# Three score tiles in the first attention too, value halves in whole tiles, and probability tiles in two pools

## The chip, the cores and the metric

The kernel runs on one core of one Trainium2 chip. The metric is the device time of one execution in microseconds; 2905.07 is the median of three executions of the kernel before. A change of about 0.2% can be told from none.

## What is computed

One block of a hybrid model, for 1024 tokens of width 1024 in fp32: a first feed-forward, a token mix, a second feed-forward, a final norm. The mix projects the normed tokens once and runs two attentions on the result. Cut to what matters here:

```python
proj = h @ w_in                                   # q, k, v of the first attention, q and six k/v of the second, gates
# first: differential attention, 8 heads, two score maps each, 128 query rows at a time
s = einsum('bqhcd,bkhcd->bhcqk', qb, k) * scale   # causal
p = softmax(s);  a = p[:, :, 0] - lam * p[:, :, 1]
o = rmsnorm(einsum('bhqk,bkhe->bqhe', a, v), head_gain) * (1.0 - lam_init)
# second: NSA, 16 heads in 2 groups: compressed, selected and window branch, mixed by gates
y_ns = g[..., 0:1] * o_cmp + g[..., 1:2] * o_slc + g[..., 2:3] * o_win
merged = sigmoid(g_a) * (y_da @ w_proj_da) + sigmoid(g_b) * (y_ns @ w_proj_nsa)
return merged @ w_out
```

## The kernel before

Everything up to the two attentions is projections and the first feed-forward. A projection is done as three products of high and low halves (`mm3`, L52 to L54: hi with whi, lo with whi, hi with wlo). So every operand is first split: ACT rounds the high half (L89), DVE subtracts it for the low half (L85). These two lines are helpers and carry many different tiles.

**The first attention** (`da_phase`) goes over eight heads and, in each, over four steps m of 256 queries, two blocks z of 128. A block has w = 128 (2m + z + 1) keys. For each block and each of the two maps, `scores` makes a score tile S on PE (L909) out of the keys kt and the queries qt, DVE adds the mask and takes the minimum nm (L916), ACT writes the exponential into a probability tile Pt (L918). POOL and DVE mix the two maps. One step later `da_pv` transposes the tiles on PE into a group tr (L964), splits it into th (ACT) and tl (DVE), and multiplies with the values vt into o (L991 to L993). `da_finish` copies o to ob and squares it to sq (ACT, L999 and L1001); `da_finish2`, a step later, sums sq on PE (tot, L1008), takes a reciprocal root by a chain of DVE, ACT (yr, yr, zr) and POOL (zr, zr, yr), scales ob on DVE (L1014), splits it into yo and stores it (syd).

Between the attention's steps stands **filler**: the projections of later heads, of gates and of the attention's output, cut into pieces (gm is their accumulator in PSUM). Weight tiles come by DMA (wst) and are split into whi and wlo, on ACT and DVE, at L1208 in the filler. `rope_pair` writes rotated queries and keys (rh, rl) to sq and sk in DRAM; `v_da_unit` transposes a head's projected values in two halves tb, splits them and stores them to sv. Keys, values and queries come back from there by DMA when their head begins (kt, vt, qt). All these DMAs are issued by one queue, SP's, one after another.

**The second attention** (`ns_phase`) is built alike: for each head and block a selected and a window score tile and their probability tiles Ps and Pw, transposed into th and tl of fp16.

**What sets the order.** The code records instructions; a scheduler then orders each engine's queue by priorities and by when pool buffers come free. The filler has a lower priority. Nothing in the code fixes where a DMA stands in SP's queue, so an edit of a pool reorders the queues around it. In the built program each engine's instructions, and SP's DMAs, stand in one fixed order.

**What the change touches.** `score_tile` has two modes. With `K.narrow`, a tile of up to 512 keys takes one PSUM bank, and there are three score tiles and three transposed groups; else a score tile takes two banks, and there are two of each. When the mode changes, both pools are closed and opened again in the other form over the same banks. Before, the first attention has `K.narrow` False and is always wide; the second is in both modes. `K.narrow` also chooses fp16 in `tr_split`. The pool mp has one buffer each of the tags rh and rl, of 4 KB a partition; a half of a head's values uses 2 KB of it. In the second attention the probability tiles are six buffers deep, in one pool.

Of the kernel before, what the change touches and what calls it, by code (L numbers as in the profile page):

```python
# [7 lines left out]
F32 = mybir.dt.float32  # L8
F32R = mybir.dt.float32r
F16 = mybir.dt.float16  # L10
# [8 lines left out]
P = 128  # L19
T = 1024  # L20
TB = 512
NTB = 2
# [21 lines left out]
def open_pool(K, ctx, name, bufs, psum=False, side=None):  # L44
    kw = {"space": PSUM} if psum else {}
    if side:
        kw["side"] = side
    return ctx.enter_context(K.tc.tile_pool(name=name, bufs=bufs, reuse_waits="tile", **kw))
# [35 lines left out]
def lo_of(nc, lo, src, hi):  # L84
    return nc.vector.tensor_tensor(out=lo, in0=src, in1=hi.bitcast(F32), op=ALU.subtract)  # L85


def split(nc, hi, lo, src):
    nc.scalar.activation(out=hi, in_=src, func=AF.Copy)  # L89
    return lo_of(nc, lo, src, hi)  # L90
# [37 lines left out]
def load_w(K, src):  # L128
    if K.fill is not None:
        return K.fill.take()  # L130
    return load_w_parts(K, src, 1)()


def load_w_parts(K, src, n):
    nc = K.nc
    st = K.wst.tile([P, KD, P], F32, tag="wst", name="wst")
    hi = K.whl.tile([P, KD, P], F32R, tag="whi", name="whi")
    lo = K.whl.tile([P, KD, P], F32R, tag="wlo", name="wlo")
    at = [0]

    def part():
        r = slice(at[0] * KD // n, (at[0] + 1) * KD // n)
        nc.sync.dma_start(out=st[:, r], in_=src[:, r])
        split(nc, hi[:, r], lo[:, r], st[:, r])
        at[0] += 1
        return hi, lo
    return part
# [495 lines left out]
def v_da_unit(K, h):  # L643
    nc = K.nc
    w = load_w(K, K.A["win"][C_VDA + h])
    for tb in range(NTB):
        ps = K.gm.tile([P, TB], F32, tag="gm", name="gm")
        yield from fill_gemm(K, ps, w, K.h[tb])
        vt = K.mp.tile([P, TB], F32, tag="m13", name="vt")
        nc.vector.tensor_tensor(out=vt, in0=ps, in1=K.R[tb], op=ALU.mult)  # L650
        tr = K.gm.tile([P, 4, P], F32, tag="gm", name="tr")
        for j in range(4):
            nc.tensor.transpose(tr[:, j], vt[:, j * P:(j + 1) * P], K.ident)
        vh = K.mp.tile([P, 4, P], F32R, tag="rh", name="vh")
        vl = K.mp.tile([P, 4, P], F32R, tag="rl", name="vl")
        split(nc, vh, vl, tr)
        for hl, t in ((0, vh), (1, vl)):
            nc.sync.dma_start(out=K.s_v[h][hl][:, tb * 4:tb * 4 + 4], in_=t.bitcast(F32))


def v_ns_unit(K, br):
# [297 lines left out]
def tr_split(K, blocks):  # L959
    nc = K.nc  # L960
    n = len(blocks) * P
    tr = K.tr.tile([P, TB], F32, tag="tr", name="tr")
    for b, src in enumerate(blocks):
        nc.tensor.transpose(tr[:, b * P:(b + 1) * P], src, K.ident)  # L964
    dt = F16 if K.narrow else F32R
    hi = K.tp.tile([P, TB], dt, tag="th", name="th")
    lo = K.tp.tile([P, TB], dt, tag="tl", name="tl")
    if K.narrow:
        nc.scalar.activation(out=hi[:, 0:n], in_=tr[:, 0:n], func=AF.Copy)  # L969
        nc.vector.tensor_tensor(out=lo[:, 0:n], in0=tr[:, 0:n], in1=hi[:, 0:n], op=ALU.subtract)  # L970
    else:
        split(nc, hi[:, 0:n], lo[:, 0:n], tr[:, 0:n])
    return hi, lo
# [104 lines left out]
def ns_scores(K, hd, m, qt, g, step):  # L1078
    nc = K.nc
    res = []  # L1080
    for i in (2 * m, 2 * m + 1):
        w = P * (i + 1)
        b0 = max(0, i - 4)
        ww = P * (i + 1 - b0)
        l = K.sm.tile([P, 2], F32, tag="l", name="l")
        nm = K.sm.tile([P, 2], F32, tag="nm", name="nm")
        qs = [t[:, (i % 4) * P:(i % 4 + 1) * P] for t in qt]
        p1 = K.pp.tile([P, 5 * P], F32, tag="P1", name="Pw")
        p0 = K.pp.tile([P, T], F32, tag="P0", name="Ps")
        scores(K, [(q, K.nk[g, 0], 0) for q in qs], w, K.slab[:, T - w:T], nm[:, 0:1], p0, l[:, 0:1])  # L1090
        mk = K.slab[:, T - ww:T] if i < 4 else K.wslab
        scores(K, [(q, K.nk[g, 1], b0 * P) for q in qs], ww, mk, nm[:, 1:2], p1, l[:, 1:2])
        nc.vector.reciprocal(out=l, in_=l)
        nc.vector.tensor_tensor(out=l, in0=l, in1=K.G[:, i, hd * 3 + 1:hd * 3 + 3], op=ALU.mult)  # L1094
        for p, n, c in ((p0, w, 0), (p1, ww, 1)):
            nc.gpsimd.tensor_scalar(out=p[:, 0:n], in0=p[:, 0:n], scalar1=l[:, c:c + 1], scalar2=P_NS,  # L1096
                                    op0=ALU.mult, op1=ALU.mult)
        res.append((p0, p1, b0))
        step()
    return res  # L1100
# [70 lines left out]
class Filler:  # L1171
# [58 lines left out]
    def step(self):  # L1230
        K = self.K
        K.gate = K.last
        self.due += self.rate
        while self.due >= 1.0 and self.done < self.target:
            self.due -= self.next()
        K.gate = None
# [102 lines left out]
def da_units(K, p):  # L1339
    return [lambda: rope_pair(K, C_QDA + 2 * p, K.s_q[p]), lambda: rope_pair(K, C_KDA + 2 * p, K.s_k[p]),  # L1340
            lambda: v_da_unit(K, 2 * p), lambda: v_da_unit(K, 2 * p + 1)]
# [15 lines left out]
B_NP = 6  # L1357
B_DT = 2
B_NT = 4
B_NO = 1  # L1360
LOW_DA = 20
LOW_NS = 100
PACE_DA = 16
# [3 lines left out]
def da_phase(K, cg):  # L1367
    nc = K.nc
    with ExitStack() as ctx:
        K.kp, K.vp, K.qp = open_pool(K, ctx, "dk", B_DK), open_pool(K, ctx, "dv", B_DV), open_pool(K, ctx, "dq", B_DQ)  # L1370
        K.nk, K.vv = {}, {}
        for n, f in enumerate(da_units(K, 0)[:2] + da_units(K, 1)):
            if n == 2:
                early = da_load_parts(K, 0)
            if n >= 2:
                next(early)
            if n == 5:
                q0 = da_queries(K, 0, 0)
            drain([f()])
        cg.close()  # L1380
        K.low = LOW_DA
        log_exp(K)
        K.pp, K.sm, K.tp, K.op = (open_pool(K, ctx, "dp", B_DP), open_pool(K, ctx, "dsm", 6), open_pool(K, ctx, "dt", B_DT),
                                  open_pool(K, ctx, "do", 1))
        K.narrow = False
        K.gm = open_pool(K, ctx, "gm1", 1, True, side="right")
        K.ops = open_pool(K, ctx, "o1", 1, True, side="right")
        pend = K.fin = None

        def finish(h, m, res):  # L1390
            if m % 2 == 0:
                K.o = K.ops.tile([P, TB], F32, tag="o", name="o")
            if K.fin:
                da_finish2(K, *K.fin)
                K.fin = None
            da_pv(K, h, m, res, K.o)
            if m % 2 == 1:
                K.fin = da_finish(K, h, m // 2, K.o)

        ng = NG_DA // 2  # L1400
        W = K.A["win"]
        units = []
        for p in (2, 3):
            cs = [[C_QDA + 2 * p, C_QDA + 2 * p + 1], [C_KDA + 2 * p, C_KDA + 2 * p + 1], [C_VDA + 2 * p], [C_VDA + 2 * p + 1]]
            units += [(f, [W[c] for c in ws]) for f, ws in zip(da_units(K, p), cs)]
        units += [(f, [W[C_GATE + c]]) for c, f in enumerate(gate_units(K, range(16)))]
        units += [(lambda d=d: pda_unit(K, d), [K.A["wda"][d]]) for d in range(KD)]
        fill = K.filler = Filler(K, units)
        for p in range(4):
            fill.pace(4 * (p + 1) if p < 2 else 8 + ng * (p - 1), PACE_DA)  # L1410
            for h in (2 * p, 2 * p + 1):
                if h:
                    da_load(K, h)
                for m in range(4):
                    qt = q0 if h + m == 0 else da_queries(K, h, m)
                    if h == 4:
                        ns_load_key(K, m)
                    res = da_scores(K, h, m, qt, fill.step)
                    if pend:
                        finish(*pend)  # L1420
                    pend = (h, m, res)
            fill.end()
        finish(*pend)
        with K.tc.high_priority(offset=-100):
            da_finish2(K, *K.fin)
        close_scores(K)


def ns_phase(K):
    nc = K.nc  # L1430
    K.low = LOW_NS
    with ExitStack() as ctx:
# [5 lines left out]
        K.kp = open_pool(K, ctx, "nk", 1)  # L1438
        K.pcp.append(open_pool(K, ctx, "npc1", 1))
        K.qp.append(open_pool(K, ctx, "nq1", 1))  # L1440
        K.tp, K.sm, K.pp, K.op = (open_pool(K, ctx, "nt", B_NT), open_pool(K, ctx, "nsm", 6), open_pool(K, ctx, "np", B_NP),
                                  open_pool(K, ctx, "no", B_NO))
        K.narrow = True
        K.gm = open_pool(K, ctx, "gm2", 1, True, side="right")
        K.ops = open_pool(K, ctx, "o2", 1, True, side="right")
        fill = K.filler
# [268 lines left out]
```

## Time and profile before

| | |
|---|---|
| median of 3 runs | 2905.07 us (2904.47 to 2907.5) |
| the profiled execution | 2906.79 us, its span 2905.0 us |
| mean granted clock of PE | 0.988 |
| PE busy in the span | 2791.6 us, 96% |
| first attention, 970 to 1478 us | PE busy 466.37 of 508, granted clock 0.97 |
| second attention, 1478 to 2068 us | PE busy 572.20 of 590, granted clock 0.99 |
| waits of PE for ACT's Pt, 970 to 1480 us | 11.1 us in 8 |
| waits of ACT's vh for the store of vh (sv) | 6.6 us in 3, the longest 5.5 |

The profile is of one execution; times are from the start of the span. In a row of the timeline stand start, length, engine, line, instruction and operands, and in brackets how long the engine had been idle before it and which instruction it then waited for. SPq is the DMA queue of SP: its length there is the issue, not the transfer. A row of waits gives the total, the number and the longest. PE's matmuls overlap, so the distance of two starts, not the length of one row, says what a matmul takes.

### The profile page before, as it was taken

The numbers are of one execution on the slowest core, as the hardware profiler recorded it, in microseconds if no ns is written. First come the engines' busy times: TensorE is split into PE (matmuls) and PEld (weight loads), VectorE is DVE, ScalarE is ACT, GpSimd is POOL, SyncE is SP. The second block draws the span as 40 slices with busy tenths as digits, with TensorE's granted clock in tenths as the row PEclk, the third lists the DMA queues.
The fourth block names the chain that finished last, engine by engine and source line by source line (L and its number), as shares of the span: only waits on it lengthen the run. The fifth ranks groups of instructions, "written<-read, shape, count | busy, mean of one in ns | idle before, by whom it ended". The sixth has DMA issues, their size and how long they took to land. (4 is left out here: it accounts for less than half of the span.)

```text
span 2905.0 us, 40199 instructions
## 1 busy us (share of the span) xinstructions
PE 2791.6 (96%) x14278; PEld 2056.3 (71%) x14278; DVE 1997.1 (69%) x3356; ACT 1371.3 (47%) x2351; POOL 785.8 (27%) x701
## 2 busy tenths in 40 slices
PE   8999999999999999989989999999999999999998
PEld 6644447887788778878867778888787854445886
DVE  7876866666688467667767777777433976676566
ACT  7533424442333245445556666677433654343443
POOL 3134321000045222322233333333242414233001
PEclk9999999999999999999999999999999999999999
DMA  4355448654446645444432226222843246444854
GB/s 163 122 201 187 168 170 279 220 182 141 152 178 213 222 150 179 164 164 159 154 121 84 89 80 204 88 88 81 311 150 123 74 148 222 162 174 170 294 181 145
DMA packets 212137, 476.12 MB, mean 164 GB/s; under 512 B 20832, under 2 KB 39520, under 8 KB 211936
## 3 DMA queue, kind: packets, MB, share of 16 engines
q1 hardware_dynamic: 211936, 473.55, 47.8%
q8 instruction: 112, 1.84, 0.3%
q14 instruction: 89, 0.73, 0.1%
HBM read 312.52 MB, written 160.96 MB: 163 GB/s over the span
## 5 line engine op out<-in xcount | busy, mean ns | idle before, releaser
L405 PEld LDWEIGHTS <-w 128*128 128x128 f16 x3024 | 297.1, 99 | 379.5 <-issue 28.6
L52 PE MATMUL gm<-hi,whi 128*128 128x512 f32 x880 | 352.2, 400 | 5.9 <-ACT whi L89 3.2
L54 PE MATMUL gm<-hi,wlo 128*128 128x512 f32 x880 | 349.2, 398 | 0.4 <-DVE wlo L85 0.3
L53 PE MATMUL gm<-lo,whi 128*128 128x512 f32 x880 | 348.8, 396 | 0.0
L405 PE MATMUL Y<-tf,w 128*128 128x512 f16 x1296 | 296.3, 383 | 17.8 <-DVE u L443 14.7
L909 PE MATMUL S<-kt,qt 128*128 128x320 f32 (+5 forms) x1152 | 268.9, 352 | 27.0 <-ACT Pt L918 11.1
L85 DVE TENSOR_TENSOR wlo<-st,whi 128x1024 fp32r<-128x1024 f32 x154 | 197.6, 1300 | 113.6 <-ACT whi L89 112.4
L916 DVE CUSTOM_DVE_ANT_0 S<-S,slab 128x896 f32<-128x896 f32 (+7 forms) x320 | 224.3, 710 | 55.6 <-PE S L909 50.6
L53 PE MATMUL acc<-wlo,whi 128*128 128x512 f32 (+1 forms) x628 | 244.1, 389 | 1.0 <-DVE wlo L85 1.0
L89 ACT ACTIVATE whi<-st 128x1024 fp32r<-128x1024 f32 x154 | 160.8, 1057 | 177.9 <-PE acc L54 110.0
L54 PE MATMUL acc<-whi,wlo 128*128 128x512 f32 (+1 forms) x628 | 242.8, 389 | 0.0
L52 PE MATMUL acc<-whi 128*128 128x512 f32 (+1 forms) x628 | 240.5, 387 | 0.0
L909 PEld LDWEIGHTS S<-kt,qt 128*128 128x128 f32 x1152 | 183.1, 190 | 43.9 <-ACT Pt L918 13.1
L970 DVE TENSOR_TENSOR tl<-tr,th 128x512 f16<-128x512 f32 (+2 forms) x304 | 183.8, 615 | 43.8 <-ACT th L969 42.5
L1096 POOL TENSOR_SCALAR Ps<-Ps,l 128x384 f32<-128x384 f32 (+7 forms) x128 | 101.1, 790 | 372.1 <-DVE l L1094 246.9
L969 ACT ACTIVATE th<-tr 128x512 f16<-128x512 f32 (+2 forms) x304 | 159.4, 540 | 79.6 <-PE tr L964 65.8
L52 PEld LDWEIGHTS gm<-hi,whi 128*128 128x128 f32 x880 | 169.0, 192 | 39.2 <-ACT whi L89 3.4
L405 PE MATMUL X<-h,w 128*128 128x512 f16 x864 | 195.3, 379 | 1.0 <-ACT s L415 1.0
L54 PEld LDWEIGHTS gm<-hi,wlo 128*128 128x128 f32 x880 | 168.4, 191 | 36.7 <-DVE wlo L85 1.5
L53 PEld LDWEIGHTS gm<-lo,whi 128*128 128x128 f32 x880 | 168.6, 192 | 30.9
L85 DVE TENSOR_TENSOR wlo<-wst,whi 128x1024 fp32r<-128x1024 f32 x103 | 138.4, 1346 | 49.4 <-ACT whi L89 39.5
L521 POOL TENSOR_TENSOR u<-u,u 128x512 f32<-128x512 f32 x36 | 52.0, 1444 | 344.3 <-DVE sa L102 162.1
(330 smaller groups left out, 6163.3 us busy)
## 6 DMA issues: line engine op xcount, KB each, us to landing
wst<-in_win_dram SPq DMA_DIRECT2D x55, 512.0 KB
sw<-w2s SPq DMA_DIRECT2D x44, 512.0 KB
st<-sw SPq DMA_DIRECT2D x88, 256.0 KB
st<-saT SPq DMA_DIRECT2D x88, 256.0 KB
a<-in_f1w_dram SPq DMA_DIRECT2D x36, 512.0 KB
a<-in_f2w_dram SPq DMA_DIRECT2D x36, 512.0 KB
st<-saB SPq DMA_DIRECT2D x66, 256.0 KB
qt<-sq SPq DMA_DIRECT2D x128, 128.0 KB
```

The source lines that it names most:

```text
L52: first = nc.tensor.matmul(out, lhsT=w[0][:, wk], rhs=x[0], start=start, stop=False, skip_group_check=skip)
L53: nc.tensor.matmul(out, lhsT=w[0][:, wk], rhs=x[1], start=False, stop=False, skip_group_check=skip)
L54: nc.tensor.matmul(out, lhsT=w[1][:, wk], rhs=x[0], start=False, stop=stop, skip_group_check=skip)
L85: return nc.vector.tensor_tensor(out=lo, in0=src, in1=hi.bitcast(F32), op=ALU.subtract)
L89: nc.scalar.activation(out=hi, in_=src, func=AF.Copy)
L405: K.mark = nc.tensor.matmul(o, lhsT=w[:, a, m * h + k], rhs=x[k][:, b], start=start and k == 0 and i == 0, stop=k == h - 1 and i == 2, ski ...
L521: nc.gpsimd.tensor_tensor(out=a, in0=a, in1=b, op=ALU.mult)
L909: K.last = nc.tensor.matmul(S[:, o:o + n], lhsT=q, rhs=k[:, k0 + c:k0 + c + n], start=i == 0, stop=i == 1)
L916: nc.vector.tensor_tensor_reduce(out=sv, in0=sv, in1=mv, scale=-0.125, scalar=BIG, op0=ALU.add, op1=ALU.min, accum_out=nm)
L969: nc.scalar.activation(out=hi[:, 0:n], in_=tr[:, 0:n], func=AF.Copy)
L970: nc.vector.tensor_tensor(out=lo[:, 0:n], in0=tr[:, 0:n], in1=hi[:, 0:n], op=ALU.subtract)
L1096: nc.gpsimd.tensor_scalar(out=p[:, 0:n], in0=p[:, 0:n], scalar1=l[:, c:c + 1], scalar2=P_NS, op0=ALU.mult, op1=ALU.mult)
```

## The change

It has three parts. (1) `v_da_unit` takes one tile for both halves of a head's high values and one for the low ones, in the same two tags, at its start, and writes each half into its part; the stores are as many and as large as before. A half then no longer waits until the first half is stored, but the next user of a tag waits for the stores of both halves. (2) The first attention sets `K.narrow` too, so its steps m = 0, 1 (up to 512 keys) are narrow and m = 2, 3 wide: two changes of the pools a head, 16 in all. A new flag `K.half` keeps the type of th and tl as it was in both phases. (3) The six probability buffers of the second attention become a pool of two and one of four, used in the same rotation; the selected tile comes ahead of the window tile in each, the pool of y goes ahead of the small one, and a pad of 1 KB shifts them in SBUF.

```diff
 def v_da_unit(K, h):
     w = load_w(K, K.A["win"][C_VDA + h])
+    vs = [K.mp.tile([P, NTB, 4, P], F32R, tag=t, name="vs") for t in ("rh", "rl")]
     for tb in range(NTB):
...
-        vh = K.mp.tile([P, 4, P], F32R, tag="rh", name="vh")
-        vl = K.mp.tile([P, 4, P], F32R, tag="rl", name="vl")
-        split(nc, vh, vl, tr)
-        for hl, t in ((0, vh), (1, vl)):
-            nc.sync.dma_start(out=K.s_v[h][hl][:, tb * 4:tb * 4 + 4], in_=t.bitcast(F32))
+        split(nc, vs[0][:, tb], vs[1][:, tb], tr)
+        for hl in range(2):
+            nc.sync.dma_start(out=K.s_v[h][hl][:, tb * 4:tb * 4 + 4], in_=vs[hl][:, tb].bitcast(F32))
@@ tr_split
-    dt = F16 if K.narrow else F32R
+    dt = F16 if K.half else F32R
...
-    if K.narrow:
+    if K.half:
@@ ns_scores
-        p1 = K.pp.tile([P, 5 * P], F32, tag="P1", name="Pw")
-        p0 = K.pp.tile([P, T], F32, tag="P0", name="Ps")
+        pool = K.pp[K.n_p % B_NP > 1]
+        K.n_p += 1
+        p0 = pool.tile([P, T], F32, tag="P0", name="Ps")
+        p1 = pool.tile([P, 5 * P], F32, tag="P1", name="Pw")
@@ da_phase
-        K.narrow = False
+        K.narrow, K.half = True, False
@@ ns_phase
-        K.tp, K.sm, K.pp, K.op = (open_pool(K, ctx, "nt", B_NT), open_pool(K, ctx, "nsm", 6), open_pool(K, ctx, "np", B_NP),
-                                  open_pool(K, ctx, "no", B_NO))
-        K.narrow = True
+        K.tp, K.op, K.sm = open_pool(K, ctx, "nt", B_NT), open_pool(K, ctx, "no", 1), open_pool(K, ctx, "nsm", 6)
+        open_pool(K, ctx, "npad", 1).tile([P, 256], F32, name="npad")
+        K.pp, K.n_p = [open_pool(K, ctx, "npa", 2), open_pool(K, ctx, "npb", B_NP - 2)], 0
+        K.narrow, K.half = True, True
```

Each engine has as many instructions as before, of the same shapes. Their order differs in the first attention and in the first steps of the second; from there on only buffer and line numbers differ. Three places follow, before and after. A number behind a name is a buffer's or a tile's.

The first is SP's queue during head 3, around a filler weight load (wst), the key loads of head 4 (kt from sk2) and the stores of a pair of rotated queries (rh, rl). Before:

```order
L1031 DMA kt_10792<-sk2_78 128x1x1024
L635 DMA sq3_75<-rh_9775 128x2x512 x2
L635 DMA sq3_75<-rl_9776 128x2x512
L1198 DMA wst_9905<-in_win_dram 128x1024
L928 DMA qt_10336<-sq1_73 128x1x256 x2
L1031 DMA kt_10794<-sk2_78 128x1x1024
L1198 DMA wst_9959<-in_win_dram 128x1024
```

After:

```order
L635 DMA sq3_75<-rh_9795 128x2x512 x2
L635 DMA sq3_75<-rl_9796 128x2x512
L927 DMA qt_10198<-sq1_73 128x1x256
L1199 DMA wst_9933<-in_win_dram 128x1024
L927 DMA qt_10198<-sq1_73 128x1x256
L927 DMA qt_10201<-sq1_73 128x1x256 x2
L1199 DMA wst_9987<-in_win_dram 128x1024
L635 DMA sq3_75<-rh_9976 128x2x512 x2
L635 DMA sq3_75<-rl_9977 128x2x512
L927 DMA qt_10369<-sq1_73 128x1x256 x2
L1030 DMA kt_10832<-sk2_78 128x1x1024
```

The weight load and the three stores now stand ahead of both key loads.

The second is around heads 3 and 4. On SP: the stores of the second half of head 6's values (sv6), the key loads of head 5 (kt from sk2) and one of the second attention's (kt from skv). Before:

```order
L1047 DMA kt_10806<-skv_84 128x1x1024
L1031 DMA kt_11307<-sk2_78 128x1x1024
L928 DMA qt_10941<-sq2_74 128x1x256 x2
L1031 DMA kt_11309<-sk2_78 128x1x1024
L658 DMA sv6_0_97<-vh_10557 128x512
L658 DMA sv6_1_98<-vl_10558 128x512
L1198 DMA wst_10577<-in_win_dram 128x1024
```

After:

```order
L657 DMA sv6_0_97<-vs_10415 128x512
L927 DMA qt_10986<-sq2_74 128x1x256
L1046 DMA kt_10846<-skv_84 128x1x1024
L657 DMA sv6_1_98<-vs_10416 128x512
L1199 DMA wst_10621<-in_win_dram 128x1024
L927 DMA qt_10989<-sq2_74 128x1x256 x2
L1030 DMA kt_11363<-sk2_78 128x1x1024
L1030 DMA kt_11365<-sk2_78 128x1x1024
```

Both stores now stand ahead of both key loads of head 5. On PE, from the last o of head 3 to the first o of head 4 (th with the new values vt). Before:

```order
L992 MATMUL o_10715<-tl_10925,vt_10166 128x128
L993 MATMUL o_10715<-th_10924,vt_10168 128x128
L909 MATMUL S_10989<-kt_10794,qt_10941 128x512 x2
L909 MATMUL S_11055<-kt_10792,qt_11044 128x320 x4
L653 MATMUL tr_10781<-ident_299,vt_10779 128x128 x4
L1008 MATMUL tot_11011<-sq_10936,ones_297 128x512
L964 MATMUL tr_11030<-ident_299,Pt_10810 128x128
L964 MATMUL tr_11030<-ident_299,Pt_10847 128x128 x2
L909 MATMUL S_11063<-kt_10794,qt_11047 128x320 x4
L964 MATMUL tr_11130<-ident_299,Pt_10948 128x128
L909 MATMUL S_11099<-kt_10792,qt_11044 128x384 x4
L991 MATMUL o_11010<-th_11034,vt_10796 128x256
```

After, the last o of head 3 is followed by 24 rows of filler on gm, of which the last two begin this piece, and the first o of head 4 comes after 18 further filler rows behind its end (22 in all behind tr):

```order
L53 MATMUL gm_10874<-lo_4958,whi_10617 128x512
L54 MATMUL gm_10874<-hi_4957,wlo_10618 128x512
L1007 MATMUL tot_11059<-sq_10984,ones_297 128x512
L963 MATMUL tr_11078<-ident_299,Pt_10850 128x128
L963 MATMUL tr_11078<-ident_299,Pt_10895 128x128 x2
L52 MATMUL gm_11015<-hi_5400,whi_10617 128x512
L53 MATMUL gm_11015<-lo_5401,whi_10617 128x512
L54 MATMUL gm_11015<-hi_5400,wlo_10618 128x512
L52 MATMUL gm_11015<-hi_5418,whi_10617 128x512
```

Before, score matmuls and transposes filled this stretch; now 46 matmuls of filler do.

The third is ACT where the second attention begins; ob, sq, yr, zr and yo are the last head's finish. Before:

```order
L89 ACTIVATE th_12889<-tr_12885 128x384
L999 ACTIVATE ob_12899<-o_12773 128x512
L1001 ACTIVATE sq_12901<-ob_12899 128x512
L155 ACTIVATE yr_12907<-m_12905 128x512
L156 ACTIVATE yr_12907<-yr_12907 128x512
L157 ACTIVATE zr_12908<-yr_12907 128x512
L89 ACTIVATE yo_12916<-ob_12899 128x512
L918 ACTIVATE Ps_12989,l_12986<-S_12996,nm_12987 128x128
L918 ACTIVATE Pw_12988,l_12986<-S_13001,nm_12987 128x128
L918 ACTIVATE Ps_13017,l_13014<-S_13018,nm_13015 128x256
L1208 ACTIVATE whi_13038<-wst_12623 128x1024
L918 ACTIVATE Pw_13016,l_13014<-S_13023,nm_13015 128x256
```

After (two more rows of Ps and Pw, of the first pair, stand just ahead of this piece):

```order
L1209 ACTIVATE whi_13149<-wst_12727 128x1024
L917 ACTIVATE Ps_13127,l_13125<-S_13129,nm_13126 128x256
L917 ACTIVATE Pw_13128,l_13125<-S_13134,nm_13126 128x256
L998 ACTIVATE ob_13003<-o_12877 128x512
L1000 ACTIVATE sq_13005<-ob_13003 128x512
L155 ACTIVATE yr_13011<-m_13009 128x512
L968 ACTIVATE th_13210<-tr_13206 128x384
L156 ACTIVATE yr_13011<-yr_13011 128x512
L968 ACTIVATE th_13222<-tr_13218 128x384
L157 ACTIVATE zr_13012<-yr_13011 128x512
L89 ACTIVATE yo_13020<-ob_13003 128x512
L917 ACTIVATE Ps_13157,l_13155<-S_13159,nm_13156 128x384
```

The exponentials of two pairs, and a weight split, moved ahead of ob; those of the third pair still stand behind yo, and two th of the second attention now stand inside the finish.

More of the change, by code (lines that the diff above doesn't have):

```diff
@@ L1359 @@
 B_NT = 4
-B_NO = 1
 LOW_DA = 20
```

## Prediction

> **What bounds the kernel now.** I read the page's busy table first, then the stretches of the differential-attention phase and its neighbours, then who waits for whom on PE there, and last the timeline at the longest of those waits.
>
> ```profile
> span 2905.0 us, 40199 instructions
> PE 2791.6 (96%) x14278; PEld 2056.3 (71%) x14278; DVE 1997.1 (69%) x3356; ACT 1371.3 (47%) x2351; POOL 785.8 (27%) x701
> ...
> 970.00:1478.00 508.00, 466.37 (x2414) 392.15 (x2413) 343.81 (x701) 237.88 (x480) 134.44 (x133) 0.97 0.48 165
> 1478.00:2068.00 590.00, 572.20 (x3872) 469.62 (x3873) 444.30 (x1148) 391.31 (x898) 186.88 (x258) 0.99 0.34 114
> 1191.00:1295.00 104.00, 89.08 (x449) 75.08 (x449) 67.75 (x143) 46.78 (x99) 28.31 (x28) 0.91 0.50 178
> 1288.00:1301.00 13.00, 10.42 (x41) 8.64 (x41) 7.62 (x13) 3.57 (x8) 5.03 (x4) 0.74 0.46 159
> ```
>
> The columns of the last four rows are the stretch, its length, the busy time of PE, PEld, DVE, ACT and POOL, the granted PE clock, the DMA share and GB/s. PE bounds the program, and the change alters neither the number nor the shape of any instruction, so time can come only from PE's idle time and from its slow clock. The first row of a stretch is the phase that the change reorders: PE stands still for 508 - 466.4 = 41.6 us, and the clock costs 508 x 0.03 = 15. Of that, the 104 us from 1191 hold 14.9 idle and 104 x 0.09 = 9.4 of clock; the next phase, whose pools the change lays out anew, idles only 17.8 in 590.
>
> ```profile
> PE S L909 <- ACT Pt L918: 11.1, 8, 5.6
> PE S L909 <- DMA kt<-sk: 4.4, 2, 4.1
> PE o L991 <- ACT th L89: 3.9, 1, 3.9
> PE o L991 <- DMA vt<-sv: 2.8, 1, 2.8
> PE S L909 <- ACT Ps L918: 8.8, 2, 8.0
> ```
>
> (The last row is of the next phase; the numbers are total, times, longest.) So the loss is a few long waits, not many short ones: one of 5.6 makes half of the eleven on score tiles. The kt wait (4.1) comes at the first head; PE's order there is alike before and after, and I leave it.
>
> **The change, place by place.** First the wait of 3.9.
>
> ```profile
> 1177.15 0.51 SPq L1031 DMA_DIRECT2D kt<-sk  x1
> 1178.37 1.06 SPq L635 DMA_DIRECT2D sq<-rh  x2
> 1180.07 0.36 SPq L635 DMA_DIRECT2D sq<-rl  x1
> 1180.47 0.90 SPq L1198 DMA_DIRECT2D wst<-in_win_dram  x1
> 1188.52 0.39 PE L52 MATMUL gm<-hi,whi 128*128 128x512 f32 x1
> 1188.75 0.39 PE L53 MATMUL gm<-lo,whi 128*128 128x512 f32 x1
> 1193.64 1.06 ACT L1208 ACTIVATE whi<-wst 128x1024 fp32r<-128x1024 f32 x1 [6.63 <-DMA wst<-in_win_dram]
> 1195.24 0.58 PE L991 MATMUL o<-th,vt 128*128 128x256 f32 x1 [3.92 <-ACT th L89]
> 1195.62 0.63 PE L52 MATMUL gm<-hi,whi 128*128 128x512 f32 x1
> 1196.05 0.63 PE L53 MATMUL gm<-lo,whi 128*128 128x512 f32 x1
> ...
> kt<-sk SPq DMA_DIRECT2D x16, 512.0 KB
> sq<-rh SPq DMA_DIRECT2D x16, 512.0 KB
> ```
>
> ACT stands before whi for a weight tile that came 13 us after its issue, behind a kt load and three stores; th is queued behind whi, and PE needs th. In the new SP order the weight load stands ahead of that kt load; the three stores stay ahead of it. So 524 KB less are in front: at the phase's 165 GB/s, 3.2 us sooner, which leaves 0.7 of the wait. The gm rows after the wait are 0.43 us apart, those before it 0.23: 13 such slow ones follow, 13 x 0.20 = 2.6 lost. After the wait of 2.76 (below) the stretch 1288 to 1301 gives 13 x 0.26 = 3.4. I take 3.0 for each of the three gaps. Gain 3.2 + 3.0 = 6.2; bounds 0 (a qt load ahead holds the queue instead) and 6.9.
>
> Next the wait of 5.6, behind a value unit's first half.
>
> ```profile
> 1247.31 0.64 SPq L1031 DMA_DIRECT2D kt<-sk  x1
> 1253.03 4.85 SPq L1031 DMA_DIRECT2D kt<-sk  x1
> 1257.98 0.42 SPq L658 DMA_DIRECT2D sv<-vh  x1
> 1270.86 0.60 ACT L89 ACTIVATE vh<-tr 128x512 fp32r<-128x512 f32 x1 [5.53 <-DMA sv<-vh]
> 1272.07 1.22 PE L909 MATMUL S<-kt,qt 128*128 128x512 f32 x2 [5.58 <-ACT Pt L918]
> ```
>
> The writer at 1270.86 is the first half of head 7's values; it waits for the store of the second half of head 6's, and Pt is queued behind it on ACT. Whole tags don't remove this wait: the next unit's first write still needs both stores of the unit before, one more than now. What removes it is the order. The stores of head 6's second half now stand ahead of both kt loads of head 5; the second of these alone holds the queue for 4.85 us. 4.85 + 0.64 = 5.5 of the 5.53, before what the two loads take on the DMA engines: gain 5.6 + 3.0 = 8.6; bounds 0 and 9.
>
> What the whole tags do remove is the wait inside a unit:
>
> ```profile
> 1285.43 0.60 ACT L89 ACTIVATE vh<-tr 128x512 fp32r<-128x512 f32 x1 [0.89 <-DMA sv<-vh]
> 1286.85 0.97 PE L909 MATMUL S<-kt,qt 128*128 128x384 f32 x4 [0.85 <-ACT Pt L918]
> 1282.33 1.49 SPq L1038 DMA_DIRECT2D vt<-sv  x2
> 1290.58 0.55 PE L991 MATMUL o<-th,vt 128*128 128x256 f32 x1 [2.76 <-DMA vt<-sv]
> ```
>
> That is worth 0.8 here. The last two rows are the wait of 2.8 at the start of head 4: its values are asked for when head 3's last o has freed their buffer, and land 8.2 us later, while PE has four transposes, tot and a dozen score matmuls. In the new order 24 + 22 projection matmuls stand between: 46 x 0.23 = 10.6 us, over the 8.2. Gain 2.8 + 3.0 = 5.8; bounds 0 and 6. Those matmuls come from what would have followed, so somewhere later 10 us less lie ready as cover; I charge 2.0 for that, about two waits like the 0.85; bounds 0 and 5.8.
>
> By the Trainium skill, "TensorE: Matmul & The Clock Gate", Part 1, the clock halves after an idle window of about 3.4 us; a gap of 2.76 would then cost no clock, and the sum below would be 3.0 less of a gain, 2895. The trace differs: the clock granted from 1288 to 1301 is 0.74 behind a gap of 2.76, so I keep the 3.0.
>
> Narrow steps: the two short query pairs of each head get three score tiles and three transposed groups, the two long ones keep two. Of the waits on Pt, 11.1 - 5.6 - 0.85 = 4.7 are left to win in both kinds together. I take 1.0, bounds 0 and 4.7. The price is 16 changes of the pools. Before shows none in this phase; the next one has them already, and there PE's waits for score tiles beside the 8.0 make 0.8. I take 0.1 a change, 1.6 in all; bounds 0 and 16 x 0.85 = 13.6, by the row at 1286.85.
>
> The two NSA pools and the pad keep six probability tiles in the same rotation; what moves is what the first ones lie over. Before, the second pair's tile lay over the last head's ob, sq and m, so it could not be written until that head was finished. Now the first two pairs lie over Pt alone.
>
> ```profile
> 1470.06 0.39 PE L992 MATMUL o<-tl,vt 128*128 128x256 f32 x1 [0.94 <-DVE tl L85]
> 1472.19 1.13 PE L1008 MATMUL tot<-sq,ones 128*128 128x512 f32 x2 [1.35 <-ACT sq L1001]
> 1479.51 0.75 DVE L1014 SCALAR_TENSOR_TENSOR ob<-ob,hgain,yr 128x512 f32<-128x512 f32 x1 [5.46 <-POOL yr L160]
> 1480.30 0.63 ACT L89 ACTIVATE yo<-ob 128x512 fp32r<-128x512 f32 x1 [4.27 <-DVE ob L1014]
> 1480.83 0.35 ACT L918 ACTIVATE Ps<-S,nm 128x128 f32<-128x128 f32 x1
> 1481.33 0.80 PE L909 MATMUL S<-kt,qt 128*128 128x256 f32 x2 [8.01 <-ACT Ps L918]
> ...
> 1275.10 0.49 ACT L89 ACTIVATE th<-tr 128x384 fp32r<-128x384 f32 x1 [1.68 <-PE tr L964]
> 1262.58 1.04 PE L964 MATMUL tr<-ident,Pt 128*128 128x128 f32 x8
> ```
>
> Today ACT stands before yo, which ends a chain of 8.1 us from tot through DVE, ACT and POOL, and the first Ps is queued behind it. In the new order four exponentials move ahead of ob, but yo still stands ahead of the third pair's Ps, and the score tile that PE wants next is the one that this Ps must empty. So the stall does not go: two th of 0.49 enter the chain, six transposes (6/8 of 1.04, 0.8) fall into the hole, and it becomes 8.0 + 1.0 - 0.8 = 8.2. What is won is the cover ahead of it: 12 projection matmuls and three score pairs now stand between the last o and tot, over the 1.35 and the 0.94 above. Net 2.3 - 0.2 = 2.1; bounds -1 (no cover won, the longer chain paid) and 13, the whole hole with its slow clock.
>
> **Sum.** Gains 6.2 + 8.6 + 0.8 + 5.8 + 1.0 + 2.1 = 24.5; costs 2.0 + 1.6. The SP queue is dealt anew in the whole phase, and its old deal left three late loads; I charge one new one at their mean, (3.9 + 5.6 + 2.8) / 3 + 3.0 = 7.1. Net gain 24.5 - 3.6 - 7.1 = 13.8. The profiled execution took 2906.79, 1.8 of it outside the span of 2905.0: 2906.8 - 13.8 = 2893. It lies 1.7 above the median of 2905.07, from which the same sum gives 2891; I say 2892, between them.
>
> **Rivals.** (1) The hole at the start of NSA goes as well. For it: nothing of finish lies under the first two pairs now. Against: ACT's order has yo ahead of the third Ps. It would bring 8.2 + 3.0 more: 2892 - 11 = 2881. Chance 0.05.
>
> (2) No change: the late loads only change places. The waits on DMA come from where a load stands in one queue, and all of that queue between the first head and NSA is dealt anew; three new late loads of 7.1 (21.3 instead of my 7.1) eat the gain up: 2892 + 14 = 2906, and with two 2899 to 2900. For it: DMA is 48% busy on average and the load at 1180 had four transfers of 512 KB ahead of it. Against: the new order has the stores and the weight load ahead at the very places that hurt. Chance 0.22.
>
> (3) Slower: the changes of the pools hold PE. The first wide score tile of a head covers the banks of three narrow tiles and of a transposed group, so PE must wait until Pt and th there are read out. If each change costs a Pt wait of 0.85 and one split of 0.60 (as vh above), 16 x 1.45 = 23.2 take the place of the 1.6: 2892 + 21.6 = 2914. At 15.4 / 16 = 0.96 each the gain is used up, and from 21.2 / 16 = 1.3 on the kernel is slower by more than 0.2%. Against: the NSA phase does the same within 0.8. For: there projection work lies between, here the exponentials are longer and ACT also splits weights. Chance 0.18.
>
> (4) The clock: short waits at every change could keep PE's clock down; at the 0.91 of the row from 1191 through all 508 us it would cost 508 x 0.06 = 30: 2922. The NSA row, with such changes, has 0.99. Chance 0.02. The Trainium skill's page "TensorE: Matmul & The Clock Gate", "A second HAM failure mode: psum-queue depth-cycling", tells of such a swing when PE cycles through banks; by the 0.99 the trace does not agree here.
>
> **How the numbers follow.** My forecast, 2892 with a range of its own of 2885 to 2899, has 0.53. A change of under 0.2% (5.8 us) can hardly be told from none. Faster by more than that: 0.53 + 0.05 = 0.58; same 0.22; slower 0.18 + 0.02 = 0.20. The range holds the forecast, rival 1 and rival 2 and leaves out 3 and 4: 2881 to 2911.
>
> **What would show it.** In the profile after: no wait of over 2 us of vh or vs for a store, no wait of o for a vt load at head 4, whi's wait for its weight tile under 4 us; still one wait of about 8 us of S for Ps at the start of NSA; the first head's 4.1 as before; granted clock of the phase 0.98 instead of 0.97, PE idle there about 25 instead of 41.6. Waits of S for Pt or th that come 16 times would speak for rival 3; new waits for kt, qt, vt or wst loads of several us for rival 2. I am wrong if the loads that I moved ahead are held up by a wait that stands in front of them in the queue, since the order shows places and no times.

## The result and the profile after

| | before | after |
|---|---|---|
| median | 2905.53 us (2904.47 to 2907.5, 4 runs) | 2946.74 us (2942.24 to 2949.97, 4 runs) |
| ratio | | 1.0138, 95% interval 1.0126 to 1.0151 |
| span of the profiled execution | 2905.0 us | 2945.6 us |
| PE busy, PE idle in that span | 2791.6, 113.4 | 2797.8, 147.8 |

The kernel became 1.4% slower; I had forecast 0.5% faster. Of the 40.6 us of span, 34.4 are idle time of PE and 6.2 busy time. PE does the same work, so I put those 6.2 down to a slower clock: the mean granted clock fell from 0.988 to 0.982. The stretches of after show where (columns as before; the second row lies inside the first):

```profile
PE 2797.8 (95%) x14278; PEld 2060.2 (70%) x14278; DVE 1999.3 (68%) x3356; ACT 1372.1 (47%) x2351; POOL 792.6 (27%) x701
...
970.00:1520.00 550.00, 476.60 (x2429) 398.98 (x2428) 347.81 (x712) 239.02 (x485) 138.65 (x135) 0.94 0.45 152
1262.00:1520.00 258.00, 210.29 (x1107) 177.91 (x1106) 155.23 (x346) 116.21 (x245) 59.08 (x64) 0.90 0.40 135
1520.00:2100.00 580.00, 560.07 (x3794) 459.88 (x3793) 435.67 (x1130) 385.69 (x884) 187.00 (x255) 0.99 0.33 109
```

It is the second half of the first attention: PE idles 47.7 us from 1262 on, at a clock of 0.90. Who waits for whom on PE, total, times and longest, from 640 to 2110 us:

```profile
PE o L990 <- DMA vt<-sv: 40.9, 5, 16.2
PE S L908 <- ACT Ps L917: 8.7, 2, 8.0
...
PE S L908 <- DMA kt<-sk: 5.5, 2, 4.2
PE gm L52 <- DVE m L626: 4.8, 5, 2.1
...
PE S L908 <- ACT Pt L917: 2.1, 5, 0.8
...
PE o L990 <- ACT th L89: 0.9, 2, 0.6
```

The waits for Pt fell from 11.1 to 2.1 and that for th from 3.9 to 0.9, as forecast. One row is new: o waits 40.9 us for the values vt of the next head, where before it waited 2.8. The timeline at the start of heads 4 and 5:

```profile
1281.85 0.28 PE L992 MATMUL o<-th,vt 128*128 128x128 f32 x1
1285.32 8.00 SPq L927 DMA_DIRECT2D qt<-sq  x4
1293.42 2.00 SPq L1046 DMA_DIRECT2D kt<-skv  x1
1296.89 0.35 SPq L1037 DMA_DIRECT2D vt<-sv  x1
1298.26 0.32 SPq L1037 DMA_DIRECT2D vt<-sv  x1
1310.54 0.55 PE L990 MATMUL o<-th,vt 128*128 128x256 f32 x1 [16.17 <-DMA vt<-sv]
1313.77 1.06 ACT L1209 ACTIVATE whi<-wst 128x1024 fp32r<-128x1024 f32 x1 [22.02 <-DMA wst<-in_win_dram]
...
1357.05 0.27 PE L992 MATMUL o<-th,vt 128*128 128x128 f32 x1
1355.89 4.89 SPq L927 DMA_DIRECT2D qt<-sq  x4
1362.66 0.88 SPq L1037 DMA_DIRECT2D vt<-sv  x2
1358.67 1.12 PE L1007 MATMUL tot<-sq,ones 128*128 128x512 f32 x2 [1.35 <-ACT sq L1000]
1371.36 0.55 PE L990 MATMUL o<-th,vt 128*128 128x256 f32 x1 [11.23 <-DMA vt<-sv]
...
1474.22 0.89 SPq L1037 DMA_DIRECT2D vt<-sv  x2
1477.96 0.35 PE L990 MATMUL o<-th,vt 128*128 128x256 f32 x1 [0.96 <-DMA vt<-sv]
```

Two things are to be seen. The load is issued late: the last o of head 3 is at 1281.85, the vt loads of head 4 go out 15 and 16 us later, behind four query loads, a key load and a value store; at head 5 they go out 5.6 us later. And at head 5 PE has nothing to do meanwhile: tot, three transposes, then o. Before, the same place reads:

```profile
1344.99 0.27 PE L993 MATMUL o<-th,vt 128*128 128x128 f32 x1
1345.18 0.80 SPq L1038 DMA_DIRECT2D vt<-sv  x2
1345.10 1.38 PE L909 MATMUL S<-kt,qt 128*128 128x320 f32 x8
1350.17 1.66 PE L909 MATMUL S<-kt,qt 128*128 128x384 f32 x8
1354.64 0.37 PE L991 MATMUL o<-th,vt 128*128 128x256 f32 x1
```

The load went out with the last o, and 16 score matmuls of step m = 2 and 24 of filler covered the 9.5 us from there to the first o. The last two rows of the fence above are the start of head 7 after the change: there PE has as little to do, but the load goes out 0.3 us behind the last o and lands in under 4, and the wait is only 1.0. So what lost cover costs depends on when the load goes out and how fast it lands. The built orders show the loss of cover. What stands between the last o of a head and the first o of the next, priced at 0.23 us for 512 columns and in proportion for fewer (the prediction's distances):

| start of head | before | after |
|---|---|---|
| 4 | 3.0 us: 14 S, 8 tr, tot | 11.0 us: 46 gm, 3 tr, tot |
| 5 | 8.6 us: 16 S, 24 gm, 6 tr, tot | 0.4 us: 3 tr, tot |
| 6 | 9.0 us: 16 S, 24 gm, 5 tr, tot | 0.4 us: 3 tr, tot |
| 7 | 9.4 us: 16 S, 24 gm, 7 tr, tot | 0.4 us: 3 tr, tot |

### The profile page after: what moved, and what is told of

It is laid out like the page before. It is cut to its first block, busy times and chain, and to the rows that moved or that the text cites. A ratio compares the mean times of both kernels' runs of the same rounds, so it can differ in the third digit from the quotient of the medians.

```text
span 2945.6 us, 40166 instructions
## 1 busy us (share of the span) xinstructions
PE 2797.8 (95%) x14278; PEld 2060.2 (70%) x14278; DVE 1999.3 (68%) x3356; ACT 1372.1 (47%) x2351; POOL 792.6 (27%) x701
## 5 line engine op out<-in xcount | busy, mean ns | idle before, releaser
L908 PEld LDWEIGHTS S<-kt,qt 128*128 128x128 f32 x1152 | 185.3, 194 | 33.8 <-ACT Ps L917 10.4
L85 DVE TENSOR_TENSOR wlo<-wst,whi 128x1024 fp32r<-128x1024 f32 x103 | 144.4, 1404 | 42.3 <-ACT whi L89 39.0
L917 ACT ACTIVATE Pt<-S,nm 128x256 f32<-128x256 f32 (+7 forms) x128 | 95.1, 744 | 126.2 <-DVE nm L915 108.9
```

The costliest lines, as they stand in the source:

```text
L908: K.last = nc.tensor.matmul(S[:, o:o + n], lhsT=q, rhs=k[:, k0 + c:k0 + c + n], start=i == 0, stop=i == 1)
L917: return nc.scalar.activation(out=pv, in_=sv, func=AF.Exp, scale=-1.0, bias=nm, accum_out=l)
```

## The experiments

My theory after the trace (C in the expectations): step m = 2 is the first wide one, so its score tile needs the banks of the narrow pools back, among them one of a transposed group of step 0 of the same head. So the scheduler puts its scores behind that step's product with the values, instead of far ahead of it; the cover between heads is gone. The rival Q: the fault lies in SP's queue alone, with the new value stores in it. P: the NSA pools.

**Parts of the change.** `e2_narrow` is before with part 2 alone; `e4_nonarrow` is after without it (the diff is that of `e4_nonarrow`):

```diff
-        K.narrow, K.half = True, False
+        K.narrow, K.half = False, False
```

> Only part 2: the first attention is narrow in its short steps; value halves and NSA pools as before. Theory C (cover): when the score pools change to wide at step m = 2, the next wide score tile lies over a transposed group of step 0, so the scheduler can no longer put the scores of step 2 between the last o of a head and the first o of the next; at heads 5 to 7 only tot and three transposes (0.4 us) are left there instead of 8.6 to 9.4, and the vt load of 8 to 9 us shows. C expects about the time of the full change, 2935 to 2950, and waits of o for vt of about 40 us in all. Theory Q (queue): the vt load stands late in SP's queue, behind query loads and the new value stores, and the whole value tags share the blame. Q expects a third or more of the loss to go, 2915 to 2932. Theory P (the NSA pools): 2890 to 2905.

> The full change with part 2 undone: whole value tags and the two NSA pools, the first attention always wide. C expects no wait of o for vt beyond the one of about 3 us of before, and 2895 to 2908. Q expects that the value stores still hold vt back, with waits of 5 us or more at several heads and 2915 or more. P expects 2930 or more.

Measured: part 2 alone 2951.38 us, ratio 1.0151 (1.0135 to 1.0166); without it 2901.87, ratio 0.9988 (0.9975 to 1.0002). So part 2 is all of the loss. The value tiles and the NSA pools are worth nothing that these runs can tell from no change. P is out, and so is the share of the whole value tags in Q.

The waits of `e2_narrow` on PE from 970 to 1520 are not those that C expected:

```profile
PE o L991 <- DMA vt<-sv: 22.5, 2, 12.3
PE gm L52 <- DVE vl L85: 20.5, 4, 14.2
```

The waits for vt are 22.5 instead of about 40. At head 4 PE waits 14.2 for vl instead, and DVE's vl waits 13.8 for the store of the half before it. So the whole value tiles did take away a wait for a store, but at head 4 a wait of 16.2 for vt took its place.

**The order alone.** `f1_tie` is before, wide, with the score matmuls of step 2 ordered behind the first o matmul of step 0:

```diff
+            mm = nc.tensor.matmul(dst, lhsT=vh, rhs=hi[:, c0:c0 + n], start=first, ...)
+            K.pv0 = mm if m + j == 0 else K.pv0
...
+            if K.tie:                          # m == 2
+                order_after(K, K.last, K.pv0)  # no semaphore, only the place on PE
```

> The kernel before (wide, halves as before, one NSA pool) with one thing added: an order, with no semaphore behind it, that puts the score matmuls of step m = 2 of each head behind the first o matmul of its step 0. In the built order 0.6 us are then left between the heads 4 to 7, as in the full change (0.4), instead of 8.6 to 9.4. Theory C (the change of the pools matters only through this order): about the time of the full change, 2930 to 2950, and waits of o for vt of 25 to 45 us. If the banks themselves, the value halves or the NSA pools cost the time: 2903 to 2912.

Measured: 2942.73 us, ratio 1.0121 (1.0106 to 1.0136), against 1.0138 for the full change. No bank, pool or store is changed here. The two rows below are its waits on PE from 970 to 1520, the others its timeline at head 5:

```profile
PE o L994 <- DMA vt<-sv: 23.9, 4, 12.9
PE S L909 <- ACT Pt L920: 12.8, 7, 5.5
...
1347.42 0.27 PE L997 MATMUL o<-th,vt 128*128 128x128 f32 x1
1349.35 5.00 SPq L930 DMA_DIRECT2D qt<-sq  x4
1356.01 0.89 SPq L1042 DMA_DIRECT2D vt<-sv  x2
1364.49 0.55 PE L994 MATMUL o<-th,vt 128*128 128x256 f32 x1 [12.89 <-DMA vt<-sv]
```

At head 5 the vt load is issued 8.6 us behind the last o here too, and the waits at heads 5 and 6 are 12.9 and 9.4 against 11.2 and 10.4. So at these heads both halves of the loss, the missing cover and the late issue, come with this order of PE, and Q is there no rival but C's second half. At head 4 the load is late as well, 11.7 us behind the last o, but PE stands there first for Pt (5.5) and for vl (4.0), and then has 11 us of filler, so it waits for vt 0.7 instead of 16.2. In all the vt waits are 23.9, a little under the 25 to 45 expected. The time is where C had it, but that it comes so close to the full change is in part luck: `f1_tie` waits less for vt and lacks what the full change gained on Pt (12.8 here, 2.1 there).

**The banks that tie.** `e5_trfixed` is after with the transposed groups in two banks of their own; only score tiles change form:

```diff
-        K.tr = open_pool(K, K.s_ctx, "tr", (3, 2)[n - 1], True)
+        if K.half:
+            K.tr = open_pool(K, K.s_ctx, "tr", (3, 2)[n - 1], True)
...
         K.narrow, K.half = True, False
+        K.tr = open_pool(K, ctx, "tr", 2, True)
```

> The full change, but in the first attention the transposed groups stay two fixed banks of their own, and only the score tiles change between three of one bank and two of two. In the built order 6 to 12 us of scores and filler stand again between the heads. C expects the vt waits to fall from 41 us to under 8, and a time of 2885 to 2900, since the gains of the other places stay. Q expects the vt waits to stay above 20 us, since the loads stand in the queue where they did, and 2925 or more.

Measured: 2925.81 us, ratio 1.0064 (1.0047 to 1.0081). The vt waits fell as C said, the time only half as far. Its waits on PE from 970 to 1520:

```profile
PE S L909 <- DMA qt<-sq: 10.9, 6, 7.1
PE o L991 <- ACT th L89: 7.7, 3, 4.4
PE gm L52 <- ACT whi L89: 7.3, 1, 7.3
PE tot L1008 <- ACT sq L1001: 6.2, 2, 4.9
PE o L991 <- DMA vt<-sv: 4.7, 3, 4.0
```

Other late DMAs took the place of vt. Two of the waits that read as waits for ACT lie behind stores, by its rows ahead of whi (where 6.0 more for POOL come between) and ahead of the longest th:

```profile
995.10 1.06 ACT L89 ACTIVATE rh<-m 128x1024 fp32r<-128x1024 f32 x1 [19.04 <-DMA sq<-rh]
1394.85 0.63 ACT L157 ACTIVATE zr<-yr 128x512 f32<-128x512 f32 x1 [9.44 <-DMA syd<-yo]
```

So query loads, a store of rotated queries and a store of a head's output now come late. That is the prediction's rival 2, with stores beside the loads, in a kernel that I had not priced it for.

**The late issue.** `e6_vtpool` is after with the vt loads on POOL's queue, in the same PE order; `f4_afterpool` moves the filler's weight loads there too; `g3_vtdouble` is after with four value buffers.

```diff
-        nc.sync.dma_start(out=t.bitcast(F32), in_=K.s_v[h][hl])     # e6, f4
+        nc.gpsimd.dma_start(out=t.bitcast(F32), in_=K.s_v[h][hl])
...
-B_DV = 2                                                            # g3
+B_DV = 4
-B_DP = 7
+B_DP = 5
```

> The full change, with the vt loads issued from POOL's queue instead of SP's, so no query load or store stands ahead of them; the matmuls keep their order, with 0.4 us of cover at heads 5 to 7 and 10.9 at head 4. C expects the wait of 16.2 at head 4 to shrink to under 4, and waits of 5 to 8 to stay at heads 5 and 6, some 2915 to 2930. Q expects all of them under 3 and 2890 to 2905.

> The full change, with the vt loads and the filler's weight loads issued from POOL's queue. The wait of 8.8 at head 4 that was left when only vt moved came from ACT standing before whi for a weight load behind the query loads. C expects that one to go, the 4.4, 4.4 and 2.4 of heads 5 to 7 to stay (cover still 0.4 us), and 2908 to 2918. Theory Q (the queue is all of it) expects every vt wait under 2 and 2890 to 2903.

> The full change with four value buffers instead of two, so that the next head's values are loaded while this head's are still in use; to make room, the probability tiles of the first attention get five buffers instead of seven. The order of the scores stays, with 0.4 us between the last o and the first o at heads 5 to 7. If the late vt loads are what the changed order costs, all waits of o for vt go and the time is 2895 to 2910, less whatever five buffers cost; if PE is held by something else in that order, it stays above 2925.

Measured: `e6_vtpool` 2925.67, ratio 1.0067 (1.0052 to 1.0082); `g3_vtdouble` 2926.36, 1.0061 (1.0047 to 1.0076); `f4_afterpool` 2931.97, 1.0079 (1.0064 to 1.0094). First `e6_vtpool` at heads 4 and 5, then one row of the waits of `g3_vtdouble` from 970 to 1520 and its head 4:

```profile
1309.12 0.58 PE L990 MATMUL o<-th,vt 128*128 128x256 f32 x1 [8.78 <-ACT th L89]
1349.56 1.13 POOL L1037 DMA_DIRECT2D vt<-sv  x2 [3.14 <-PE o L992]
1356.60 0.55 PE L990 MATMUL o<-th,vt 128*128 128x256 f32 x1 [4.44 <-DMA vt<-sv]
```

```profile
PE o L990 <- ACT th L89: 12.2, 6, 9.6
...
1309.79 1.06 ACT L1209 ACTIVATE whi<-wst 128x1024 fp32r<-128x1024 f32 x1 [19.68 <-DMA wst<-in_win_dram]
1311.90 0.58 PE L990 MATMUL o<-th,vt 128*128 128x256 f32 x1 [9.55 <-ACT th L89]
```

At head 5 the wait fell from 11.2 to 4.4 when the load went out on time: 6.8 of it were the queue, 4.4 the missing cover. At head 4, where C had expected under 4 of `e6_vtpool`, the wait stays at 8.8 and 9.6 although vt comes early: ACT stands before whi for a weight tile that is as late as vt was, and th is queued behind it. With four buffers every wait for vt is gone, and half of the loss stays, above all in that wait and in key loads. The expectation of 2895 to 2910 failed and the sign for the other case, over 2925, came: vt is about half of what the order costs. No run has the five probability buffers of `g3_vtdouble` alone, so their share is open; but `e6_vtpool`, which keeps seven, comes to the same time. `f4_afterpool` was expected near 2913, for its weight loads are on time. The wait of 8.8 went and 4.3 and 4.4 stayed at heads 5 and 6, as expected, but waits for queries rose from 4.0 to 8.7 and the time is no better than that of `e6_vtpool`. Its profile has a granted clock of 0.96 in the first 400 us, where the kernels don't differ and before has 1.00; why is open, so I read nothing from its time.

**Towards a faster kernel.** `f3_trfixed_pool` joins the fixed groups with both loads on POOL's queue. `f2_wide_pool` does it with the wide version. From `f2_wide_pool`, `g1_svpool` moves the value stores to POOL's queue, `g2_tail` does the last head's scaling and split into yo on POOL, and `g12_both` does both.

```diff
-    order_after(self.K, self.K.nc.sync.dma_start(out=st, in_=self.srcs[n]), self.last)    # f2, f3: weights, vt as in e6
+    order_after(self.K, self.K.nc.gpsimd.dma_start(out=st, in_=self.srcs[n]), self.last)
...
+    if last:                                                                              # g2, g12
+        nc.gpsimd.tensor_scalar(out=ob, in0=ob, scalar1=K.hgain[:, h:h + 1], ...)
+        nc.gpsimd.tensor_tensor(out=ob, in0=ob, in1=y, op=ALU.mult)
...
+        nc.gpsimd.tensor_scalar(out=yo[0], in0=ob, scalar1=1.0, scalar2=1.0, ...)
+        nc.gpsimd.tensor_tensor(out=yo[1], in0=ob, in1=yo[0].bitcast(F32), op=ALU.subtract)
```

> The transposed groups fixed (cover of 7 to 12 us between all heads) and both kinds of load on POOL's queue, the value halves and NSA pools of the full change. Both C and Q expect no vt wait over 2; C with Q, as two parts of one loss, expects 2885 to 2905. If it stays above 2915, the loss of the version with fixed groups (2926) is of another kind, in what else the SP queue carries.

> The first attention wide, value halves and NSA pools of the full change, both kinds of load on POOL's queue. The waits of 3.7 (th behind whi) and 3.4 (vt) that the wide version still has should fall under 1, that of 6.4 behind the value store should stay: 2887 to 2899. If POOL's own work is held up by the issues instead: 2902 or more.

> The wide version with vt and filler weights on POOL's queue, and the stores of the value halves on POOL's queue too. If the wait of 6.1 behind the value store comes from where that store stands in SP's queue (behind two key loads), it falls under 2 and the time is 2882 to 2893 against 2895 before this edit. If POOL's own work ahead of the store holds it up as long: 2893 to 2899.

> The wide version with vt and filler weights on POOL's queue; in the last head's finish the scaling and the split into yo are done on POOL alone, so neither ACT nor DVE stands before the end of that chain. In ACT's order the third pair's Ps now comes right behind zr. If ACT standing before yo is what makes the 7.4 us hole at the start of NSA, it falls to 3 to 4.5 and the time by 3 to 6: 2889 to 2893. If the probability scaling on POOL, now behind the longer chain, holds PE instead: 2895 or more.

> The last two edits together. If both work and are independent, their gains add: 2878 to 2888. If the value stores on POOL meet the same POOL work, less than their sum.

| kernel | median us | ratio to before |
|---|---|---|
| `f3_trfixed_pool` | 2918.69 | 1.0031 (1.0018 to 1.0045) |
| `f2_wide_pool` | 2895.29 | 0.9959 (0.9944 to 0.9974) |
| `g1_svpool` | 2902.51 | 0.9983 (0.9974 to 0.9993) |
| `g2_tail` | 2900.36 | 0.9971 (0.9962 to 0.9981) |
| `g12_both` | 2902.78 | 0.9983 (0.9974 to 0.9992) |

Before took 2909.74 us beside the first two and 2907.52 beside the others, so the ratios are what to compare. All but `f3_trfixed_pool` are faster than before by their intervals, `g1_svpool` and `g12_both` by less than 0.2%. Only `f2_wide_pool` came out in the range expected if the edit works; the wide version without POOL's queue, `e4_nonarrow`, had 0.9988. In `f3_trfixed_pool` no wait for vt of note is left, and it is still slower than before; what is left (7.5 us of gm for whi, 6.3 of S for qt, 4.9 of tot for sq at the longest) I have not taken apart. In `f2_wide_pool` the wait of th is gone, that of 3.4 for vt fell only to 2.9. Of the single edits: the longest waits of S in `g1_svpool`, and the first NSA waits in `g2_tail`, from 970 to 1520:

```profile
PE S L908 <- DMA qt<-sq: 13.6, 5, 10.9
PE S L908 <- ACT Pt L917: 6.4, 6, 3.4
```

```profile
PE S L908 <- ACT Pt L917: 12.2, 8, 6.4
PE tr L963 <- POOL Ps L1105: 2.5, 1, 2.5
PE S L908 <- ACT Ps L917: 2.5, 1, 2.5
```

Moving the value stores took the 6.1 behind vs away and brought one of 10.9 for a query load; the 3.4 that is left is another wait, 2.7 in `f2_wide_pool`, behind a store of rotated keys. The tail on POOL cut the hole of 7.4 to 2.5, but 2.5 came back behind POOL's probability scaling, and nothing of it shows in the ratio: the expected 3 to 6 us were not measured. The two together gain nothing over `f2_wide_pool` either.

## Why the prediction was wrong, point by point

- **Where it failed: the cover at the start of a head.** The step "46 x 0.23 = 10.6 us, over the 8.2. Gain 2.8 + 3.0 = 5.8" has two errors. The 8.2 ran from issue to landing, and I let the issue stand with the last o. In the new queue it stood behind four query loads and came 15 us later, and then the load took 13.6 us to land, so the wait grew to 16.2 instead of vanishing. (I also read "four transposes" and "a dozen" score matmuls as the cover of before; it was 8 and 14, which changes nothing.) And I looked at head 4 only, because the trace of before has its vt wait there. At heads 5 to 7 before has no such wait since 8.6 to 9.4 us of work covered the load; the new order took that to 0.4. A place without a wait in the profile is where a reordering can cost most.
- **The term for lost cover was mis-sized.** I charged 2.0 for the filler moved away; heads 5 and 6 alone wait 11.2 and 10.4, and PE's busy time grew by 6.2 us, which I put down to the slow clock behind the waits.
- **Rival 3 had the place, not the way.** It named the wide tile over the narrow tiles and a transposed group, and priced it as 16 waits of PE for Pt and th. There are no 16 such waits: S waits for Pt 2.1 in all, in 5. The scheduler had settled the conflict in the order, by putting the scores later, and it was paid at another instruction, as a wait for a load.
- **Rival 2 was real and too small.** Late loads did change places, but to 16, 11 and 10 us instead of 4.1 (7.1 with the clock), since the load and its cover moved at once. 2911 was no upper end.
- **The value units:** no wait of vs for a store of values, as forecast; but `e4_nonarrow` shows that the order which did it came with part 2. Undoing that brings a wait of 6.4 for Pt back. In the new order PE waits 14.2 at head 4 with the halves of before (`e2_narrow`).
- **The weight load at head 3:** th no longer waits there (0.9 instead of 3.9). At head 4 ACT's wait for a weight tile came back, 22 us long; there it costs nothing beside the wait for vt, until vt comes early (`e6_vtpool`: 8.8).
- **Third score tile:** I took 1.0 of 4.7; 2.1 of waits for Pt are left, so 2.6 at most; the order changed as well, and no run has the third tile alone.
- **NSA pools:** the hole was to stay near 8.2, and it did, at 8.0; tot's 1.35 and o's 0.94 for tl were to be covered, and they were: the last head's tot starts without a wait. The waits of 1.35 for sq that after shows stand at heads 5 to 7, where the cover was lost. With the wide first attention the hole is 7.4.
- **Clock:** it was to rise to 0.98 and fell to 0.94. By the Trainium skill, "TensorE: Matmul & The Clock Gate", Part 1, idle gaps of over about 3.4 us halve the clock for a while; the 0.90 from 1262 on, with three gaps of 10 to 16 us, agrees. The gap of 2.76 that the prediction went by, with its 0.74, is shorter than that.

## What to carry to other kernels

When pools that a scheduler reads share banks, ask which later work an early buffer now has to wait behind: the cost may show at another engine as a late load, with no wait at the tile itself. Before a reordering, list for each load what covers it now, also where the profile shows no wait, and count the same between the same two instructions in the new order. A load's cover starts at its issue, so look at the queue ahead of it as well.

## What the runs showed of the hardware

The SP queue was more than a place to issue from. In the built program the DMAs of that queue use eight semaphores in turn, and most of them (1164 of 1421) carry a wait until the one eight places ahead has landed. The four query loads at 1285.32 are among these, their waits for PE were over by 1282, and they held the queue for 8.0 us. By the Trainium skill, "DMA: Bandwidth & Descriptors", "Issuing engines are not separate DMA queues", issuing from several engines saves only the sequencer's usually small time. Here the same loads from POOL's queue cut a wait from 11.2 to 4.4, and in the wide kernel, with the weights, the ratio went from 0.9988 to 0.9959. That is more than this sentence of the Trainium skill leads one to expect: the transfers share the engines, but not the place in line.
